# Recurrence: masked copies into a zeroed tile, and the decayed keys on VectorE

## The chip, the core and the metric

The program runs on one core of a Trainium2 chip. The metric is the device time of one execution in microseconds (us); of several executions the median is given. The engines of the core are TensorE (PE in the profile, PEld its weight loads), VectorE (DVE), ScalarE (ACT), GpSimd (POOL) and SyncE (SP, which here issues DMAs).

## The reference

Two transformer blocks on 512 tokens of width 1024, all in float32. The change lies in one of the three branches of the second block, a gated recurrence with four heads of 128 keys and 128 values (`hgrn2_mixer`):

```
b = jnp.cumsum(lfc, axis=2)
o_inter = jnp.einsum('bhck,bhkv->bhcv', qc * jnp.exp(b), state)
diff = b[:, :, :, None, :] - b[:, :, None, :, :]
decay = jnp.exp(jnp.where(causal, diff, NEG_BIG))
attn = jnp.einsum('bhtk,bhsk,bhtsk->bhts', qc, kc, decay)
o_intra = jnp.einsum('bhts,bhsv->bhtv', attn, vc)
```

Here `lfc` is the logarithm of the forget gate. The score `attn` of a token t with an earlier token s sums over keys a product of query, key and the decay between s and t. The reference goes in chunks of 64; the kernel takes chunks of 128.

## The kernel before

The decay between two tokens can't be split into a factor of t and a factor of s that are both safe to compute over a whole chunk. So the kernel splits the 128 x 128 scores of a chunk by seven levels (blocks of 2, 4, ... 128 tokens): at each level the pairs with s in the first half of a block and t in the second are exact with respect to the block's middle. An eighth part is the diagonal. Each pair (s, t) belongs to one level alone, so the scores are the sum over the eight parts, each under a mask of zeros and ones.

The class `Hgrn` does this. `mix` goes over 16 steps, one for each chunk i (4) and head h (4):

- `logs`: for two heads at a time, TensorE transposes the log gates, ScalarE and VectorE split them into a high and a low part (`fh`, `fl`).
- `decays`: TensorE multiplies them with a constant matrix `lev` (lines 1661 and 1662), ScalarE takes the exponential into `E`, nine tiles of 128 x 128 (line 1663). Tiles 0 to 6 times the keys are `yk` (GpSimd, line 1665); tile 8 times the keys is `kd` (line 1670); then tiles 0 to 7 are multiplied by the queries in place (VectorE, line 1672). Line 1672 overwrites what line 1665 reads, so it has to wait for it.
- `mixed`: TensorE forms the eight products (lines 1682 and 1684) into two PSUM tiles `s` of four each; VectorE multiplies each tile by its masks (line 1685) and adds the eight to one (lines 1686 to 1688) in the tile `am`.
- `put`: TensorE multiplies `am` with the values (line 1696), adds the state's part (line 1698), and the new state `hst` is formed (lines 1701 to 1709).

The steps overlap: while the `decays` of a step are computed, `mixed` works on the step before it and `put` on the one before that. The three PSUM tiles named `s` are shared with `scores` (lines 717 and 718), the indexer of another branch, which leaves its results on VectorE in `ixs` (lines 1313, 1316 and 1317). A generator `merge` hands out pieces of this and of projections (`pj`, lines 216 to 218, each weight split by ScalarE into `whi` and by VectorE into `wlo`, line 203) between the steps. After them `topk` (lines 1327 and 1328, 48 rounds of a maximum and a replacement on VectorE) selects the keys of another branch; its result is wanted only much later.

The order of each engine's instructions is set when the program is built, by a scheduler that goes by priorities and its own estimates. On the chip each engine takes its instructions in that order; semaphores make them wait for each other.

Of the kernel before, what the change touches and what calls it, by code (L numbers as in the profile page):

```python
# [10 lines left out]
F32 = mybir.dt.float32  # L11
F32R = mybir.dt.float32r
BF16 = mybir.dt.bfloat16
I32 = mybir.dt.int32
AF = mybir.ActivationFunctionType
ALU = mybir.AluOpType
AX = mybir.AxisListType
# [3 lines left out]
P = 128  # L21
# [13 lines left out]
class Net:  # L35
# [200 lines left out]
    def rsqrt(self, y, x, n, eng=None):  # L236

        eng = eng or self.nc.vector
        yi = self.t("rs_i", [P, 16], 3, I32)[:, :n]
        (self.nc.vector if eng is self.nc.scalar else eng).tensor_scalar(yi, x.bitcast(I32), -0.5, float(0x5F3759DF - 0x400000 - 2 ** 31), op0=ALU.mult, op1=ALU.add)  # L240
        u = yi.bitcast(F32)
        v = self.t("rs_t", [P, 16], 3)[:, :n]
        for it in range(3):
            o = y if it == 2 else u
            if eng is self.nc.scalar:
                eng.activation(v, u, AF.Identity, scale=u)
                eng.activation(v, v, AF.Identity, scale=x, bias=self.m15)
                eng.activation(o, v, AF.Identity, scale=u)
                continue
# [16 lines left out]
    def root(self, y, s, n, eps, x):  # L266

        nc = self.nc
        ln = nc.scalar.activation(y, s, AF.Ln, scale=1.0 / n, bias=self.eps[eps])
        self.after(ln, self.table)  # L270
        nc.scalar.activation(y, y, AF.Exp, scale=-0.5)
        nc.vector.tensor_scalar(x, s, -0.5 / n, -0.5 * eps, op0=ALU.mult, op1=ALU.add)
# [32 lines left out]
    def layernorm(self, x, g, b, eps, mv, sums=True):  # L305

        nc = self.nc
        if sums:
            nc.vector.tensor_scalar(mv[:, 2:3], mv[:, 0:1], mv[:, 1:2], -1.0 / D, op0=ALU.add, op1=ALU.mult)
            sq = self.wa([P, D], BF16)  # L310
            nc.scalar.activation(sq, x, AF.Square, bias=mv[:, 2:3], accum_out=mv[:, 3:4])
            self.root(mv[:, 5:6], mv[:, 3:4], D, eps, mv[:, 4:5])
# [639 lines left out]
    def tables2(self, tab):  # L952

        nc, a = self.nc, self.a
        pi = self.wp(dt=I32)
        nc.scalar.dma_start(pi, a["positions_2"].broadcast_to([P, S]))
# [23 lines left out]
    def bias2(self, pool):  # L980
# [1 line left out]


        nc, a = self.nc, self.a
        U32 = mybir.dt.uint32
        self.bias = [self.dr.tile([P, 4, (i + 1) * P], F32, name=f"bias{i}") for i in range(NT)]
        slot = lambda dt=F32, shape=None: pool.tile(shape or [P, S], dt, name=self.nm("bt"), tag="bt", bufs=6)
        hot = lambda: pool.tile([P, S], F32R, name=self.nm("bh"), tag="bh", bufs=2)
# [1 line left out]
        pos = a["positions_2"]  # L990
        pi = slot(I32)
        nc.sync.dma_start(pi, pos.broadcast_to([P, S]))
        qi = self.t("b_qi", [P, 3, NT], 1, I32)
        nc.sync.dma_start(qi[:, 0], pos[0].rearrange("(t p) -> p t", p=P))
# [10 lines left out]
        ps = self.p("s")  # L1005
# [9 lines left out]
        def part(src, op, arg, out):  # L1015
            k = slot(I32)[:, :src.shape[1]]
            nc.vector.tensor_single_scalar(k, src, arg, op=op)
            nc.vector.tensor_copy(out, k)
            return out
# [8 lines left out]
        for h in range(4):  # L1028
            raw = pool.tile([P, 2, 256], F32, name=self.nm("bo"), tag="bo", bufs=3)
            x = tab[h]  # L1030
            nc.sync.dma_start(raw, bass.AP(x.tensor, x.offset, [[1, P], [P, 2], [1, 256]]))
            f = self.split(raw.rearrange("p a b -> p (a b)"), slot)
            for r in range(2):
                ps = self.p("s")
                for k, y in enumerate((0, 0, 1, 1)):
                    z = k % 2
# [27 lines left out]
        for i in range(NT):  # L1064
            w = (i + 1) * P
            ps = pool.tile([P, 4 * S], F32, name=self.nm("bq"), tag="bq")
# [522 lines left out]
class Hgrn:  # L1589


    def __init__(self, net, hT, col):
        self.net, self.nc, self.hT, self.col = net, net.nc, hT, col
        nc, a = net.nc, net.a
        self.la, self.l1, self.kc, self.gb = net.bounds
        self.lev = net.sub.tile([P, 9, P], F32R, name="lev", tag="lev")
        nc.gpsimd.dma_start(self.lev, a["c_lev"])
        self.lmask = net.sub.tile([P, 8, P], BF16, name="lmask", tag="lmask")
        nc.gpsimd.dma_start(self.lmask, a["c_lmask"])
        self.bi = net.bi  # L1600
        self.f = net.sub.tile([P, 4, S], F32, name="hf", tag="hf")
        self.kT = []
# [34 lines left out]
    def mix(self, qT):  # L1637

        net, nc = self.net, self.nc
        kT, lev, lmask = self.kT, self.lev, self.lmask  # L1640
        st = [None] * 4
        self.os = [net.slot(shape=[P, 4, P]) for _ in range(4)]
        bq = lambda x, ti, n: x[:, ti].rearrange("p (o t) -> p o t", o=1).broadcast_to([P, n, P])
        pvs = {}

        def logs(i, hp):
            ti = slice(i * P, (i + 1) * P)
            pt = net.p("tr", [P, 4, P])[:, 0:2]
            for h in range(2):
                nc.tensor.transpose(pt[:, h, :], self.f[:, hp + h, ti], net.ident)  # L1650
            fh, fl = (self.w(t, [P, 2, P], 2, F32R) for t in ("fh", "fl"))
            nc.scalar.copy(fh, pt)
            nc.vector.tensor_sub(fl, pt, fh)
            return fh, fl

        def decays(i, h, fh, fl):
            ti = slice(i * P, (i + 1) * P)
            E = self.E()
            for c in range(0, 9, 3):
                ps = net.p("s", [P, 4, P])[:, :3, :]  # L1660
                nc.tensor.matmul(ps, lhsT=fh[:, h % 2, :], rhs=lev[:, c:c + 3, :], start=True, stop=False)
                nc.tensor.matmul(ps, lhsT=fl[:, h % 2, :], rhs=lev[:, c:c + 3, :], start=False, stop=True)
                nc.scalar.activation(E[:, c:c + 3, :], ps, AF.Exp)
            yk = self.w("yk", [P, 7, P], 2)
            nc.gpsimd.tensor_mul(yk, E[:, :7, :], bq(kT[h], ti, 7))
            kd = dec = None
            if i < NT - 1:
                kd = self.w("kd", [P, 2, P], 2)
                dec = net.t("hdec", [P, 1], 4)
                nc.vector.tensor_mul(kd[:, 0, :], E[:, 8, :], kT[h][:, ti])  # L1670
                nc.vector.tensor_copy(dec, E[:, 7, 127:128])
            nc.vector.tensor_mul(E[:, :8, :], E[:, :8, :], bq(qT[h], ti, 8))
            return E, yk, kd, dec

        def mixed(i, h, E, yk, kd, dec):
            ti = slice(i * P, (i + 1) * P)
            am = [self.w("am", [P, 4, P], 4) for _ in range(2)]
            for c in (0, 4):
                ps = net.p("s", [P, 4, P])
                for l in range(4):  # L1680
                    if c + l < 7:
                        nc.tensor.matmul(ps[:, l, :], lhsT=yk[:, c + l, :], rhs=E[:, c + l, :], start=True, stop=True)
                    else:
                        nc.tensor.matmul(ps[:, l, :], lhsT=kT[h][:, ti], rhs=qT[h][:, ti], start=True, stop=True)
                nc.vector.tensor_mul(am[c // 4], ps, lmask[:, c:c + 4, :])
            nc.vector.tensor_add(am[0], am[0], am[1])
            nc.vector.tensor_add(am[0][:, 0:2], am[0][:, 0:2], am[0][:, 2:4])
            nc.vector.tensor_add(am[0][:, 0], am[0][:, 0], am[0][:, 1])
            return i, h, E, am[0], kd, dec

        def put(i, h, E, am, kd, dec):
            if h == 0:
                pvs[i] = net.p("pv", [P, 4, P])
            pv = pvs[i]
            vv = self.bi[:, i, h * P:(h + 1) * P]
            nc.tensor.matmul(pv[:, h, :], lhsT=am[:, 0], rhs=vv, start=True, stop=i == 0)
            if i > 0:
                nc.tensor.matmul(pv[:, h, :], lhsT=E[:, 7, :], rhs=st[h], start=False, stop=True)
            if i < NT - 1:
                p2 = net.p("tr", [P, 4, P])  # L1700
                nc.tensor.transpose(p2[:, 0, :], kd[:, 0, :], net.ident)
                nc.scalar.copy(kd[:, 1, :], p2[:, 0, :])
                p3 = p2[:, 1, :]
                nc.tensor.matmul(p3, lhsT=kd[:, 1, :], rhs=vv, start=True, stop=True)
                new = self.w("hst", [P, P], 5)
                if i == 0:
                    nc.vector.tensor_copy(new, p3)
                else:
                    nc.vector.scalar_tensor_tensor(new, st[h], dec, p3, op0=ALU.mult, op1=ALU.add)
                st[h] = new  # L1710
            if h == 3:
                for j in range(4):
                    nc.scalar.copy(self.os[j][:, i], pv[:, j])

        held = prods = None
        f = logs(0, 0)
        for i in range(NT):
            for h in range(4):
                if h % 2 == 0:
                    g = f  # L1720
                d = decays(i, h, *g)
                if held:
                    m = mixed(*held)
                    if prods:
                        put(*prods)
                    prods = m
                held = (i, h) + d
                if h % 2 == 0 and (i, h) < (NT - 1, 2):
                    f = logs(i + h // 2, 2 - h)
                yield  # L1730
        m = mixed(*held)
        put(*prods)
        put(*m)
        yield
# [95 lines left out]
```

## Time and profile before

| | |
|---|---|
| time, median of 3 runs | 1677.36 us (1676.02 to 1679.92) |
| the profiled execution's own time | 1676.82 us |
| its span in the profile | 1675.1 us |
| granted clock of TensorE, mean | 0.995 of full speed |
| TensorE busy | 1618.9 us, 97% of the span |
| VectorE busy | 1056.8 us, 63% |
| ScalarE busy | 734.6 us, 44% |
| GpSimd busy | 105.7 us, 6% |

TensorE is busy nearly all the time, so the time of the kernel is TensorE's work and its waits. Shares over the whole span say little of one stage: the recurrence runs from about 770 to 906 us of the span, and there the other engines are loaded quite otherwise.

### The profile page before, as it was taken

How to read it: one execution, taken by the hardware profiler on the slowest of the kernel's cores; microseconds unless marked ns; L12 is line 12 of the kernel's file. 1: busy time of each engine (PE TensorE's matmuls, PEld its weight loads, DVE VectorE, ACT ScalarE, POOL GpSimd, SP SyncE). 2: the span in 40 equal slices, each digit the busy share in tenths (PEclk: the TensorE clock that was granted, in tenths of full speed). 3: DMA queues.
4: the chain of work that ended last, by engine and by line, in shares of the span. 5: the costliest groups of instructions: out<-in, count | busy, mean ns of one | idle time of the engine just before them, and what ended most of it. 6: DMA issues, size and time to landing. Idle time of an engine off the chain costs nothing.

```text
span 1675.1 us, 24263 instructions
## 1 busy us (share of the span) xinstructions
PE 1618.9 (97%) x9320; PEld 1374.6 (82%) x9320; DVE 1056.8 (63%) x2281; ACT 734.6 (44%) x1507; POOL 105.7 (6%) x131
## 2 busy tenths in 40 slices
PE   6999999999999999899889999999999999999997
PEld 6878797987787889787778866788889988888997
DVE  7686779784578796747999995624355444343233
ACT  4455664443465643465443765522233222222222
POOL 1021000000000000002221001100000000000000
PEclk9999999999999999999999999999999999999999
DMA  7453032341121414332011320223432533333321
GB/s 229 141 167 109 26 116 74 101 152 51 51 76 39 148 55 126 121 100 64 26 30 49 93 76 27 91 91 108 144 120 101 176 101 101 101 101 95 95 90 62
DMA packets 141883, 160.06 MB, mean 96 GB/s; under 512 B 14100, under 2 KB 131108, under 8 KB 141256
## 3 DMA queue, kind: packets, MB, share of 16 engines
q1 hardware_dynamic: 135960, 141.34, 28.0%
q0 software_dynamic: 2944, 11.86, 2.1%
q10 hardware_dynamic: 2864, 5.32, 1.0%
q8 instruction: 73, 1.20, 0.3%
q14 instruction: 42, 0.34, 0.1%
HBM read 143.55 MB, written 15.21 MB: 95 GB/s over the span
## 4 chain that ended last, share of the span: by engine, by line
PE 76%; DVE 13%; ACT 3%; issue 2%; DMA 1%; POOL 1%; ACTq 0%; POOLq 0%
PE pj L217 18%; PE pj L218 18%; PE pj L216 18%; PE pv L1093 3%; PE s L216 2%; PE s L217 2%; PE s L218 2%; PE tr L731 2%; DVE wlo L203 2%; PE s L717 1%; PE s L836 1%; PE s L718 1%; DVE ixs L1313 1%; DMA wraw<-in_w_in_dram 1%; ACT whi L202 1%
## 5 line engine op out<-in xcount | busy, mean ns | idle before, releaser
L216 PE MATMUL pj<-hTh,whi 128*128 128x512 f32 (+1 forms) x1136 | 440.5, 388 | 0.0
L217 PE MATMUL pj<-hTl,whi 128*128 128x512 f32 (+1 forms) x1136 | 440.3, 388 | 0.0
L218 PE MATMUL pj<-hTh,wlo 128*128 128x512 f32 (+1 forms) x1136 | 439.8, 388 | 0.3 <-DVE wlo L203 0.3
L203 DVE TENSOR_TENSOR wlo<-wraw,whi 128x1024 fp32r<-128x1024 f32 (+3 forms) x237 | 271.9, 1153 | 240.1 <-ACT whi L202 236.3
L202 ACT CAST whi<-wraw 128x1024 fp32r<-128x1024 f32 (+3 forms) x237 | 229.1, 980 | 327.1 <-PE pj L217 193.5
L216 PEld LDWEIGHTS pj<-hTh,whi 128*128 128x128 f32 x1136 | 213.6, 188 | 45.4 <-issue 6.6
L217 PEld LDWEIGHTS pj<-hTl,whi 128*128 128x128 f32 x1136 | 213.6, 188 | 43.4 <-issue 4.7
L218 PEld LDWEIGHTS pj<-hTh,wlo 128*128 128x128 f32 x1136 | 213.6, 188 | 43.2 <-issue 3.8
L216 PE MATMUL pj<-whi,hTh 128*128 128x256 f32 (+2 forms) x352 | 101.1, 289 | 3.4 <-ACT whi L207 2.7
L218 PE MATMUL pj<-whi,hTl 128*128 128x256 f32 (+2 forms) x352 | 102.5, 292 | 0.0
L217 PE MATMUL pj<-wlo,hTh 128*128 128x256 f32 (+2 forms) x352 | 101.2, 288 | 0.0
L217 PE MATMUL pj<-wlo,t2k 128*128 128x256 f32 x304 | 85.9, 283 | 0.0
L218 PE MATMUL pj<-whi,t2k 128*128 128x256 f32 x304 | 85.7, 282 | 0.0
L216 PE MATMUL pj<-whi,t2k 128*128 128x256 f32 x304 | 85.3, 281 | 0.0
L216 PE MATMUL s<-whi,t2k 128*128 128x256 f32 x264 | 73.8, 280 | 0.0
L218 PE MATMUL s<-whi,t2k 128*128 128x256 f32 x264 | 73.8, 280 | 0.0
L217 PE MATMUL s<-wlo,t2k 128*128 128x256 f32 x264 | 73.8, 280 | 0.0
L216 PEld LDWEIGHTS pj<-whi,hTh 128*128 128x128 f32 x352 | 68.2, 194 | 5.1 <-ACT whi L207 3.3
L217 PEld LDWEIGHTS pj<-wlo,hTh 128*128 128x128 f32 x352 | 68.4, 194 | 0.5 <-DVE wlo L203 0.2
L218 PEld LDWEIGHTS pj<-whi,hTl 128*128 128x128 f32 x352 | 68.3, 194 | 0.4
L734 ACT COPY wa<-tr 128x128 f32<-128x128 f32 (+3 forms) x96 | 40.7, 424 | 58.8 <-PE tr L731 57.4
L722 DVE CUSTOM_DVE_ANT_0 wa<-s,mask 128x128 f32<-128x128 f32 (+3 forms) x112 | 52.5, 485 | 11.4 <-PE tr L731 7.9
(455 smaller groups left out, 3120.2 us busy)
## 6 DMA issues: line engine op xcount, KB each, us to landing
wraw<-in_w_in_dram SPq DMA_DIRECT2D x112, 512.0 KB, 3.8
wraw<-in_w_ffn_gate_dram SPq DMA_DIRECT2D x22, 512.0 KB, 3.9
wraw<-in_w_ffn_up_dram SPq DMA_DIRECT2D x22, 512.0 KB, 4.6
wraw<-in_w_ffn_down_dram SPq DMA_DIRECT2D x16, 512.0 KB, 3.6
tok<-hres SPq DMA_DIRECT2D x12, 512.0 KB, 7.7
wraw<-in_w_out_dram SPq DMA_DIRECT2D x12, 512.0 KB, 4.3
hres<-tok SPq DMA_DIRECT2D x12, 512.0 KB, 2.7
wraw<-in_w_out_dram SPq DMA_DIRECT2D x8, 384.0 KB, 3.0
```

What stands on the lines that cost most here:

```text
L202: nc.scalar.copy(hi[:, ka:kb], raw)
L203: nc.vector.tensor_sub(lo[:, ka:kb], raw, hi[:, ka:kb])
L216: nc.tensor.matmul(out, lhsT=wh(k), rhs=xh(k), start=start and k == 0, stop=False)
L217: nc.tensor.matmul(out, lhsT=wh(k), rhs=xl(k), start=False, stop=False)
L218: nc.tensor.matmul(out, lhsT=wl(k), rhs=xh(k), start=False, stop=stop and k == nk - 1)
L717: nc.tensor.matmul(sc, lhsT=stacked[:, rows], rhs=twice[hh][:, cols], start=True, stop=False)
L718: return nc.tensor.matmul(sc, lhsT=stacked[:, rows], rhs=twice[2 + hh][:, cols], start=False, stop=stop)
L722: self.nc.vector.tensor_tensor_reduce(p[:, :w], sc[:, :w], self.maskw[:, S - w:] if mask is None else mask, scale=1.0, scalar=3e38, op0=AL ...
L731: x = nc.tensor.transpose(pt[:, j, :], src[:, j * P:(j + 1) * P], self.ident)
L734: nc.scalar.copy(dst[:, :n, :], pt[:, :n, :])
L836: last = nc.tensor.matmul(sc[:, S - wj:], lhsT=m, rhs=y[:, end - wj:end], start=n == 0, stop=n == len(todo) - 1)
L1093: x = self.nc.tensor.matmul(out, lhsT=l, rhs=r, start=k == 0, stop=k == i)
```

## The change

Two things are changed. First, VectorE no longer multiplies the products by masks and adds two tiles of four. It copies the products under the masks into a tile of zeros: two fixed tiles `am`, set to zero once by GpSimd, take turns from step to step. A place (s, t) in them is always written at the same level, so that what is not written stays zero. The second copy goes into the same tile as the first, and the first of the three additions (512 columns) falls away; the other two now write to `ay` and `az`. The masks are kept in float32 and not in bfloat16, and are read as integers. Second, line 1665 is given to VectorE.

```
-        self.lmask = net.sub.tile([P, 8, P], BF16, name="lmask", tag="lmask")
+        self.lmask = net.sub.tile([P, 8, P], F32, name="lmask", tag="lmask")
+        self.am = [net.sub.tile([P, 4, P], F32, name=f"am{j}", tag=f"am{j}") for j in range(2)]
+        for x in self.am:
+            nc.gpsimd.memset(x, 0.0)
...
-            nc.gpsimd.tensor_mul(yk, E[:, :7, :], bq(kT[h], ti, 7))
+            nc.vector.tensor_mul(yk, E[:, :7, :], bq(kT[h], ti, 7))
...
-            am = [self.w("am", [P, 4, P], 4) for _ in range(2)]
+            am = self.am[(i * 4 + h) % 2]
...
-                nc.vector.tensor_mul(am[c // 4], ps, lmask[:, c:c + 4, :])
-            nc.vector.tensor_add(am[0], am[0], am[1])
-            nc.vector.tensor_add(am[0][:, 0:2], am[0][:, 0:2], am[0][:, 2:4])
-            nc.vector.tensor_add(am[0][:, 0], am[0][:, 0], am[0][:, 1])
-            return i, h, E, am[0], kd, dec
+
+                nc.vector.copy_predicated(am, lmask[:, c:c + 4, :].bitcast(U32), ps)
+            y = self.w("ay", [P, 2, P], 1)
+            z = self.w("az", [P, 1, P], 3)
+            nc.vector.tensor_add(y, am[:, 0:2], am[:, 2:4])
+            nc.vector.tensor_add(z[:, 0], y[:, 0], y[:, 1])
+            return i, h, E, z, kd, dec
```

VectorE has as many instructions as before, GpSimd 16 products fewer and two fills more. The scheduler also puts other instructions in another order.

The first place is VectorE's queue in an early step of the recurrence. A row gives the line, the operation, the tile written, the tiles read and the size; the numbers behind the names are those of buffers. Before:

```order
L1671 COPY hdec_7890<-E_7874 128x1
L1685 TENSOR_TENSOR am_7894<-s_7896,lmask 128x512
L1313 SCALAR_TENSOR_TENSOR ixs_7860<-wa_7871,iw_6746,ixs_7860 128x384
L1670 TENSOR_TENSOR kd_7889<-E_7874,t2k_7493 128x128
L1672 TENSOR_TENSOR E_7874<-E_7874,t2k_7571 128x1024
L1685 TENSOR_TENSOR am_7895<-s_7902,lmask 128x512
L1707 COPY hst_7916<-tr_7912 128x128
L1686 TENSOR_TENSOR am_7894<-am_7894,am_7895 128x512
L1316 TENSOR_SCALAR ixs_7918<-wa_7922,iw_6746 128x384
L1687 TENSOR_TENSOR am_7894<-am_7894 128x256
L1317 SCALAR_TENSOR_TENSOR ixs_7918<-wa_7922,iw_6746,mask 128x128
L1688 TENSOR_TENSOR am_7894<-am_7894 128x128
```

And of the change, whose line numbers are up to five higher there:

```order
L1668 TENSOR_TENSOR yk_7889<-E_7876,t2k_7497 128x896
L1673 TENSOR_TENSOR kd_7891<-E_7876,t2k_7497 128x128
L1674 COPY hdec_7892<-E_7876 128x1
L1689 COPY_PREDICATED am_7281<-lmask,s_7896 128x512
L1675 TENSOR_TENSOR E_7876<-E_7876,t2k_7575 128x1024
L1689 COPY_PREDICATED am_7281<-lmask,s_7902 128x512
L1712 COPY hst_7917<-tr_7913 128x128
L1692 TENSOR_TENSOR ay_7908<-am_7281 128x256
L1316 TENSOR_SCALAR ixs_7919<-wa_7923,iw_6746 128x384
L1693 TENSOR_TENSOR az_7909<-ay_7908 128x128
L1317 SCALAR_TENSOR_TENSOR ixs_7919<-wa_7923,iw_6746,mask 128x128
```

`yk` now stands at the head of the step, and `kd` has moved up behind it, so that both stand ahead of the first masked copy; the addition of 512 columns is gone.

The second place is VectorE's queue near the end of the recurrence, where rounds of `topk` (MAX and MATCH_REPLACE) stand between the steps. Before:

```order
L1688 TENSOR_TENSOR am_8676<-am_8676 128x128
L1328 MATCH_REPLACE ixs_7794<-ixm_10085,ixs_7794 128x256
L1327 MAX ixm_10104<-ixs_7794 128x8
L1328 MATCH_REPLACE ixs_7794<-ixm_10104,ixs_7794 128x256
L1327 MAX ixm_10185<-ixs_7794 128x8
L1328 MATCH_REPLACE ixs_7794<-ixm_10185,ixs_7794 128x256
L1327 MAX ixm_10213<-ixs_7794 128x8
L1328 MATCH_REPLACE ixs_7794<-ixm_10213,ixs_7794 128x256
L1327 MAX ixm_10234<-ixs_7794 128x8
L203 TENSOR_TENSOR wlo_8941<-wraw_8942,whi_8940 128x1024
L1742 SCALAR_TENSOR_TENSOR t2k_8730<-t2k_8730,pj_8705 128x512
L1685 TENSOR_TENSOR am_8749<-s_8751,lmask 128x512
```

And of the change:

```order
L1693 TENSOR_TENSOR az_8681<-ay_8680 128x128
L1327 MAX ixm_9919<-ixs_7797 128x8
L1328 MATCH_REPLACE ixs_7797<-ixm_9919,ixs_7797 128x256
L1327 MAX ixm_9935<-ixs_7797 128x8
L1328 MATCH_REPLACE ixs_7797<-ixm_9935,ixs_7797 128x256
L1327 MAX ixm_9952<-ixs_7797 128x8
L1328 MATCH_REPLACE ixs_7797<-ixm_9952,ixs_7797 128x256
L1327 MAX ixm_9969<-ixs_7797 128x8
L1328 MATCH_REPLACE ixs_7797<-ixm_9969,ixs_7797 128x256
L1327 MAX ixm_10028<-ixs_7797 128x8
L204 TENSOR_TENSOR wlo_8929<-wraw_8930,whi_8928 128x1024
L1747 SCALAR_TENSOR_TENSOR t2k_8721<-t2k_8721,pj_8696 128x512
```

Before, eleven of the 48 rounds begin ahead of the last masked product; of the change five begin ahead of the last masked copy, the first of them at this place. Six rounds have moved behind the recurrence.

## Rows read from the trace of the kernel before

**Rows 1.** Page, part 1: busy us (share of the span) xinstructions.
```profile
PE 1618.9 (97%) x9320; PEld 1374.6 (82%) x9320; DVE 1056.8 (63%) x2281; ACT 734.6 (44%) x1507; POOL 105.7 (6%) x131
```
**Rows 2.** Busy time by engine in three stretches, the recurrence first.
```profile
core 0: us, PE busy (x) PEld busy (x) DVE busy (x) ACT busy (x) POOL busy (x), PEclk, DMA share, GB/s
780.00:900.00 120.00, 104.76 (x627) 87.89 (x625) 111.57 (x197) 51.15 (x115) 33.90 (x14) 1.00 0.12 32
900.00:1000.00 100.00, 98.05 (x585) 84.35 (x585) 97.05 (x249) 66.75 (x190) 3.31 (x4) 1.00 0.28 81
1000.00:1100.00 100.00, 98.97 (x496) 71.31 (x496) 55.12 (x171) 47.49 (x134) 11.19 (x12) 1.00 0.18 56
```
**Rows 3.** TensorE's waits, 780 to 902 us: us in total, times, longest.
```profile
PE pv L1696 <- DVE hdec L1671: 3.1, 2, 1.9
PE s L717 <- DVE am L1685: 2.6, 2, 1.4
PE s L1661 <- DVE am L1685: 2.2, 3, 0.9
PE tr L1650 <- DVE hst L1709: 2.0, 2, 1.5
PE s L1682 <- DVE E L1672: 1.9, 2, 1.1
PE tr L1701 <- DVE fl L1653: 1.6, 1, 1.6
PE pv L1696 <- DVE am L1688: 1.6, 1, 1.6
...
```
**Rows 4.** VectorE's waits, 760 to 910 us (two of five groups).
```profile
DVE E L1672 <- POOL yk L1665: 7.0, 6, 2.0
DVE kd L1670 <- ACT E L1663: 0.8, 2, 0.4
```
**Rows 5.** Timeline from 808 us: start, us, engine, instruction, [idle before it <-releaser].
```profile
808.29 2.47 POOL L1665 TENSOR_TENSOR yk<-E,t2k 128x896 f32<-128x896 f32 x1 [3.56 <-ACT E L1663]
808.73 2.44 DVE L1313 SCALAR_TENSOR_TENSOR ixs<-wa,iw,ixs 128x384 f32<-128x384 f32 x1
811.44 0.41 DVE L1653 TENSOR_TENSOR fl<-tr,fh 128x256 fp32r<-128x256 f32 x1
811.90 0.33 PE L1701 MATMUL tr<-ident,kd 128*128 128x128 f32 x1 [1.57 <-DVE fl L1653]
811.97 0.60 DVE L1313 SCALAR_TENSOR_TENSOR ixs<-wa,iw,ixs 128x384 f32<-128x384 f32 x1
```
**Rows 6.** Groups by shape, VectorE, 765 to 910 us: xcount | busy us, mean ns | idle before.
```profile
L1685 DVE TENSOR_TENSOR am<-s,lmask 128x512 f32<-128x512 f32 x32 | 21.6, 680 | 0.2
L1672 DVE TENSOR_TENSOR E<-E,t2k 128x1024 f32<-128x1024 f32 x16 | 19.5, 1218 | 7.0 <-POOL yk L1665 7.0
L203 DVE TENSOR_TENSOR wlo<-wraw,whi 128x1024 fp32r<-128x1024 f32 x10 | 13.5, 1353 | 5.6 <-ACT whi L202 5.5
L1686 DVE TENSOR_TENSOR am<-am,am 128x512 f32<-128x512 f32 x16 | 12.3, 771 | 0.0
L1313 DVE SCALAR_TENSOR_TENSOR ixs<-wa,iw,ixs 128x384 f32<-128x384 f32 x7 | 9.8, 1402 | 0.0
L1313 DVE SCALAR_TENSOR_TENSOR ixs<-wa,iw,ixs 128x256 f32<-128x256 f32 x7 | 8.9, 1274 | 0.0
L1327 DVE MAX8 ixm<-ixs 128x8 f32<-128x256 f32 x13 | 5.5, 426 | 0.3
L1328 DVE MATCH_REPLACE8 ixs<-ixm,ixs 128x256 f32<-128x256 f32 x12 | 4.9, 409 | 0.0
```
**Rows 7.** Timeline of VectorE: a single line 1313 of 256 columns.
```profile
805.60 0.47 DVE L1313 SCALAR_TENSOR_TENSOR ixs<-wa,iw,ixs 128x256 f32<-128x256 f32 x1
```
**Rows 8.** Groups by shape, VectorE, whole span: masked copies of another stage.
```profile
L1072 DVE COPY_PREDICATED bo<-b_n,bq 128x512 f32<-128x512 uint32 x4 | 2.7, 747 | 0.0
```
**Rows 9.** Timeline of VectorE from 125 us: three of these copies in a row.
```profile
125.40 2.00 DVE L1072 COPY_PREDICATED bo<-b_n,bq 128x512 f32<-128x512 uint32 x3
```

More of the change, by code (lines that the diff above doesn't have):

```diff
@@ L14 @@
 I32 = mybir.dt.int32
+U32 = mybir.dt.uint32
 AF = mybir.ActivationFunctionType
@@ L984, in bias2 @@
         nc, a = self.nc, self.a
-        U32 = mybir.dt.uint32
         self.bias = [self.dr.tile([P, 4, (i + 1) * P], F32, name=f"bias{i}") for i in range(NT)]
```

## The prediction

> **What bounds the kernel now.** I read the page first: TensorE is busy for 97% of the span, VectorE for 63% [rows 1]. So only what makes TensorE wait can be worth anything, and I looked for the stretches where it does. The windows show one inside the span: from 780 to 900 us, most of the recurrence, TensorE is busy for 104.8 of 120 us, so it idles 15.2, while VectorE is busy for 111.6 [rows 2]. In the 100 us behind it TensorE idles only 2.0, although VectorE is busy for 97.0 there, and in the 100 after that VectorE is half idle. In the recurrence, then, VectorE is the engine that TensorE waits for, and the waits say so themselves: all of the groups in the stretch name VectorE as the releaser, and the seven shown add up to 15.0 us [rows 3]. They name different lines (`hdec`, `am`, `hst`, `E`, `fl`). That is the mark of an engine that is late as a whole, whatever stands in its queue when TensorE asks.
>
> Then I asked why VectorE is late, and its groups by shape gave a second answer besides its load. Line 1313 has a mean of 1402 ns for 384 columns and of 1274 ns for 256 [rows 6]; single ones of these shapes take 0.60 [rows 5] and 0.47 us [rows 7]. The timeline shows what stretches them: at 808.73 one of 384 columns starts while GpSimd is at work on `yk`, and takes 2.44 us, that is, it ends shortly after GpSimd does at 810.76; `fl` behind it is late, and TensorE waits 1.57 us for `fl` [rows 5]. Besides, VectorE waits 7.0 us outright for `yk`, since line 1672 overwrites what GpSimd still reads [rows 4].
>
> **The change, part by part.** All of it lies between 770 and 906 us; sums are for the 16 steps.
>
> The addition of 512 columns goes. It is 16 instructions with a mean of 771 ns: 12.3 us off VectorE [rows 6]. Of these 1.5 us are holds by GpSimd, measured against 680 ns of the masked product of as many columns.
>
> GpSimd's products go, and with them the holds and the waits. The holds of the other groups: line 1313, 7 x (1402 - 600) = 5.6 us and 7 x (1274 - 470) = 5.6 us; line 203, 10 x (1353 - 1218) = 1.4 us, with line 1672, of as many columns, for the normal length [rows 5 to 7]. Together 12.6 us. With the 7.0 us of waits for `yk` [rows 4] VectorE gets 19.6 us back here.
>
> `yk` comes onto VectorE: 896 columns, two inputs in SBUF. Between the 680 ns for 512 columns and the 1218 ns for 1024 [rows 6], a line gives 680 + 384 x 538 / 512 = 1083 ns, so 17.3 us for 16. This is a price from both sides, and I give it no range of its own.
>
> The masked products become masked copies, 32 of them. The trace has this operation elsewhere, at the same width with all operands in SBUF: 747 ns on the mean [rows 8], and 2.00 us for three in a row, or 0.67 each [rows 9]. The source is now in PSUM, which no row shows for this operation; the masked product reads the same tile from PSUM in 680 ns, as if it cost nothing. Against 680 ns the 32 copies change the sum by -0.3 to +2.1 us. I take 0, by the copies in a row, since VectorE's queue is full here too.
>
> Masks of four bytes in place of two, and two fills by GpSimd: the masks are loaded and the tiles filled before the recurrence, while GpSimd has nothing else to do and TensorE goes on with projections, and I put it at nothing. Were that cover gone, it would be a few us, once.
>
> So VectorE's account is -12.3 - 19.6 + 17.3 = -14.6 us (-14.9 to -12.5), against 15.2 us for which TensorE idles. This is the core of the forecast: the engine that is late becomes earlier by nearly as much as it makes the other wait.
>
> Here the Trainium skill has a rule that speaks against the change. Its page "Perfetto Trace Analysis", section "Optimizing Scalar/DVE Operations", says that when the vector engine is saturated, moving work to ScalarE or even GpSimd may make sense, and adds that the two share a read port, so that it might not help. By its first half the change gives work back to a full engine, -12.3 + 17.3 = +5.0 us, and the time would come to 1682. The page "SBUF — State Buffer", section "Who interferes with whom", says that the shared port is held for a whole instruction and the other engine blocks fully; the instruction at 808.73 agrees with that. The sums above don't use either.
>
> **What TensorE gets of it.** Not all 14.6. First, by what is left of the load: VectorE's busy time from 780 to 900 falls by about 12.3 + 12.6 - 17.3 = 7.6 us to 104, and six rounds of `topk`, each 426 + 409 ns [rows 6], move behind the recurrence, so 99, against TensorE's 104.8. Two queues that are so nearly equal and wait for each other leave some idle time. Its bounds: the 2% of the stretch behind, with VectorE as full [rows 2], give 2 us; 13% as now give 15. I take 5 us, a third of today's, nearer to the low end because TensorE's present waits come each from a hold or wait of 1 to 2 us that disappears. I followed all 15 back in the timeline as in [rows 5]; 13 have one just ahead of them. That gives 15.2 - 5 = 10.2 us.
>
> Second, the six rounds, 5.0 us, now load a stretch in which VectorE has 3.0 us free; what doesn't fit runs over into the next, where it has 45 [rows 2], and nothing urgent waits for `topk`. I set 0.5 us for work of VectorE that stands behind these rounds in the queue and is awaited.
>
> Third, the new order itself: the first masked copy of a step now stands behind `yk` and `kd`. I count that in the 5 us.
>
> 10.2 - 0.5 = 9.7 us. The profiled execution took 1676.8 us, of which 1675.1 are the span, so 1667.1; the median lies 0.5 above this execution: **1667.5 us**.
>
> **Rivals.** *All of it comes back.* TensorE idles for 2 us in the recurrence, as in the stretch behind it, and a little is won as its pipeline drains less often: 14 to 16 us, 1662. For it: the holds are the larger half of VectorE's lateness. Against it: 99 us of work in about 107 is still 93%.
>
> *VectorE stays the late engine; no change.* `yk` now waits in VectorE's own queue for the exponentials; on GpSimd that wait was free, and it was long (3.56 us of idle time before the `yk` of [rows 5]). While VectorE waits at its head, everything behind it waits too. For about 0.8 us in each step, 13 us would go. Against it: `hdec` and `kd` stood in the same queue before and read the same tile, and VectorE waited for `E` only 0.8 us in all [rows 4]. The time would be 1676.
>
> *Slower: the tiles `s`.* The first masked copy of a step comes later by `yk` and `kd`, and until it has run TensorE can't have that PSUM tile again; there are three. The waits for them are 2.6 + 2.2 us in five cases today [rows 3]. If in each step TensorE stood still for all of `yk`, that is 16 x 1.08 = 17.3 us; with copies at 747 ns 2.1 more. Against the 15.2 won, that gives +4 us: 1681. It decides from 15.2 / 16 = 0.95 us a step. Against it: in between, TensorE has projections to do, which the new order puts there in larger number. The rule of the saturated engine, +5.0 us with the holds left out of account, ends in the same place by another way, 1682; the trace bears it out least, as VectorE demonstrably stands still under GpSimd's products.
>
> **How the numbers follow.** Forecast (5 to 14 us faster) 0.62; all of it 0.12; no change 0.15; slower 0.11, of which the saturated engine 0.03. The measurement can tell about 0.2%, or 3.4 us, from no change. Faster by more is the first two, 0.74; within it 0.15; slower 0.11. The likeliest case alone spans 1663 to 1672. The range has to take in most of the case without change and part of the case in which all comes back: 1661 to 1677. It leaves out the slower case and the outermost of the others.
>
> **What would show it right or wrong.** In the profile after: `yk` on VectorE at 1.0 to 1.15 us; masked copies at 0.66 to 0.75; lines 1313 at 0.60 and 0.47 us throughout, with no instruction of VectorE near 2 us; no wait for `yk`; VectorE busy for about 100 us of the 120 that begin at 780; TensorE idle for about 5 us in the recurrence, which ends some 10 us earlier; TensorE's idle time behind it as before. I am wrong if copies from PSUM take a microsecond and more, if TensorE's waits for `am` (tiles `s`) grow to 15 us, if VectorE stands before `yk` waiting for ScalarE's `E`, or if the displaced `topk` makes TensorE wait past 906 us.

## The result: 1.1% faster, 1660.4 us

The changed kernel takes 1660.37 us (median of four runs, 1657.14 to 1661.47), the kernel before 1678.44 us beside it. The ratio is 0.9891, with a 95% interval of 0.9871 to 0.9910: 18 us faster. The forecast was 1667.5 us with a range from 1661 to 1677, so the time lies just below the range. The direction was right, the size too small. The profiled execution took 1661.47 us (span 1659.7), which is 15.3 us less than the 1676.8 of before.

Part 1 of the page of the changed kernel answers to [rows 1]:

```profile
PE 1618.0 (97%) x9320; PEld 1374.3 (83%) x9320; DVE 1045.5 (63%) x2281; ACT 734.5 (44%) x1507; POOL 67.0 (4%) x117
```

TensorE has the same work, and VectorE does 11 us less although it took over 16 products. The windows of the changed kernel over the same stretches as [rows 2], the recurrence first:

```profile
core 0: us, PE busy (x) PEld busy (x) DVE busy (x) ACT busy (x) POOL busy (x), PEclk, DMA share, GB/s
780.00:900.00 120.00, 119.86 (x769) 104.42 (x768) 112.49 (x227) 57.30 (x141) 0.00 (x0) 1.00 0.14 41
900.00:1000.00 100.00, 98.15 (x511) 77.63 (x509) 94.48 (x250) 66.70 (x185) 2.28 (x4) 0.98 0.24 71
1000.00:1100.00 100.00, 99.47 (x501) 75.01 (x502) 49.56 (x144) 44.80 (x117) 11.02 (x12) 1.00 0.23 72
```

From 780 to 900 us TensorE idles for 0.14 us, where it was 15.2. Its list of waits over the stretch of [rows 3] is empty. The stretch behind idles as before (1.85 and 1.95 us), so the stall didn't move there. Its granted clock is 0.98 where it was 1.00: in this trace TensorE ran at 0.50 (1.2 GHz) from 965 to 968 us, behind a wait of 1.9 us for ScalarE's `ms`. The kernel before has a wait of 1.8 us there and kept 1.00.

A fixed window holds a different part of the program once the stage is shorter. For the comparisons from here on I take the stage itself, from the first matmul on `lev` to the last of `put` (line 1696, now 1701). One row of the windows view for the kernel before, columns as above:

```profile
769.70:906.20 136.50, 121.19 (x736) 103.06 (x736) 124.73 (x225) 55.86 (x125) 38.33 (x16) 1.00 0.14 39
```

And the same row for the changed kernel:

```profile
770.60:890.40 119.80, 119.66 (x742) 103.11 (x741) 110.45 (x208) 56.01 (x125) 0.00 (x0) 1.00 0.15 45
```

The stage is 16.7 us shorter: TensorE's idle time in it falls from 15.31 (136.50 - 121.19) to 0.14, and its own work there takes 1.5 us less. The stage begins 0.9 us later, and what follows it takes 0.4 us longer, together 15.4 us off the span. Note VectorE: 124.73 of 136.50 is 91%, 110.45 of 119.80 is 92%. It is as full as before, and TensorE no longer waits.

VectorE's groups by shape in the changed kernel, 765 to 910 us, for [rows 6]:

```profile
L1689 DVE COPY_PREDICATED am<-lmask,s 128x512 f32<-128x512 uint32 x32 | 23.6, 742 | 0.7 <-PE s L1685 0.6
L1675 DVE TENSOR_TENSOR E<-E,t2k 128x1024 f32<-128x1024 f32 x16 | 19.5, 1216 | 0.0
L1668 DVE TENSOR_TENSOR yk<-E,t2k 128x896 f32<-128x896 f32 x16 | 17.4, 1090 | 0.9 <-ACT E L1666 0.8
L204 DVE TENSOR_TENSOR wlo<-wraw,whi 128x1024 fp32r<-128x1024 f32 x12 | 14.7, 1225 | 5.6 <-ACT whi L203 5.6
...
L1313 DVE SCALAR_TENSOR_TENSOR ixs<-wa,iw,ixs 128x384 f32<-128x384 f32 x7 | 4.3, 611 | 0.0
...
L1327 DVE MAX8 ixm<-ixs 128x8 f32<-128x256 f32 x8 | 3.4, 429 | 0.2
L1313 DVE SCALAR_TENSOR_TENSOR ixs<-wa,iw,ixs 128x256 f32<-128x256 f32 x7 | 3.4, 485 | 0.0
...
L1328 DVE MATCH_REPLACE8 ixs<-ixm,ixs 128x256 f32<-128x256 f32 x7 | 2.9, 418 | 0.0
```

Line 1313 is down to 611 and 485 ns from 1402 and 1274, line 204 (203 before) to 1225 from 1353, and the 7.0 us of waiting ahead of `E` are 0.0. A masked copy from PSUM has its first price: 742 ns, against 680 for the product in its place.

VectorE's timeline at the place of [rows 5], in the changed kernel:

```profile
808.35 0.61 DVE L1313 SCALAR_TENSOR_TENSOR ixs<-wa,iw,ixs 128x384 f32<-128x384 f32 x1
808.88 1.08 DVE L1668 TENSOR_TENSOR yk<-E,t2k 128x896 f32<-128x896 f32 x1
809.96 0.29 DVE L1673 TENSOR_TENSOR kd<-E,t2k 128x128 f32<-128x128 f32 x1
810.17 0.14 DVE L1674 COPY hdec<-E 128x1 f32<-128x1 f32 x1
810.24 0.74 DVE L1689 COPY_PREDICATED am<-lmask,s 128x512 f32<-128x512 uint32 x1
810.87 1.21 DVE L1675 TENSOR_TENSOR E<-E,t2k 128x1024 f32<-128x1024 f32 x1
```

In the 2.44 us that line 1313 alone took, VectorE now does line 1313, `yk`, `kd`, `hdec` and most of a masked copy.

### The profile page after: what moved, and what is told of

It reads as the page before. It is cut to its first block, busy times and chain, and to the rows that moved or that the text cites. A ratio compares the mean times of both kernels' runs of the same rounds, so it can differ in the third digit from the quotient of the medians.

```text
span 1659.7 us, 24221 instructions
## 1 busy us (share of the span) xinstructions
PE 1618.0 (97%) x9320; PEld 1374.3 (83%) x9320; DVE 1045.5 (63%) x2281; ACT 734.5 (44%) x1507; POOL 67.0 (4%) x117
## 4 chain that ended last, share of the span: by engine, by line
PE 83%; DVE 8%; ACT 2%; DMA 1%; issue 1%; ACTq 0%; DVEq 0%
PE pj L218 19%; PE pj L217 19%; PE pj L219 19%; PE pv L1093 3%; PE tr L732 2%; PE s L217 2%; PE s L218 2%; PE s L219 2%; PE s L718 2%; PE s L1685 2%; PE s L719 1%; PE s L837 1%; DVE wlo L204 1%; DMA wraw<-in_w_in_dram 1%; PE pv L848 1%
```

## The experiments

Two things left VectorE at once: the time that GpSimd's products cost it (holds of 15.1 us in nine instructions, by each one's length above the shortest of its kind; a tenth, the only one of its kind, a line 1316 of 256 columns, took 2.17 us and takes 0.34 in the changed kernel; and the 7.0 us of [rows 4]) and the addition of 512 columns. My first theory, A, was that GpSimd's products are what matters; its rival, B, that VectorE's load as a whole is. The letters are explained in each expectation. Times are medians, ratios are against the kernel before on the same chip, and the stage is that of the section above.

**Half of the change: `yk` alone.** The kernel before, with one word changed:

```diff
-            nc.gpsimd.tensor_mul(yk, E[:, :7, :], bq(kT[h], ti, 7))
+            nc.vector.tensor_mul(yk, E[:, :7, :], bq(kT[h], ti, 7))
```

> Edit: of the change, only the keys' product goes to VectorE; masked products and all three additions stay as before. Theory A (single holds: TensorE's waits in the recurrence come from the 1 to 2 us that VectorE stands still under each of GpSimd's products; without them even a nearly full VectorE keeps up): the holds (14.1 us) and the waits (7.0 us) are gone, VectorE has the addition of 512 columns more per step than in the change, so a few us of TensorE's idle time are left, 2 to 5; time 1662 to 1666. Theory B (load: only VectorE's account counts, which is -14.1 - 7.0 + 17.3 = -3.8 us here): 1674 to 1676.

Measured: 1668.46 us, ratio 0.9952 (0.9937 to 0.9967). It lies between the two, nearer to A: putting 17 us of work on the engine that TensorE waits for makes the kernel 0.5% faster. Here the Trainium skill's advice is answered ("Perfetto Trace Analysis", section "Optimizing Scalar/DVE Operations": with a saturated vector engine, offloading even to GpSimd may make sense, but the two share a read port). The run goes against the first half and with the caution. The stage of this kernel:

```profile
770.40:899.80 129.40, 124.79 (x750) 106.33 (x750) 118.23 (x218) 56.26 (x125) 0.00 (x0) 0.99 0.13 37
```

TensorE still idles for 4.61 us, and its work in the stage takes 124.79 us instead of 119.66. Of these 5.1 us, 3.8 are also in the whole span (1621.8 against 1618.0 busy). The windows of this kernel show a part of them, in the column PEclk:

```profile
856.00:858.00 2.00, 1.11 (x4) 0.60 (x4) 2.00 (x6) 0.74 (x2) 0.00 (x0) 1.00 0.00 0
858.00:859.00 1.00, 0.12 (x1) 0.00 (x0) 1.00 (x2) 0.49 (x1) 0.00 (x0) 1.00 0.00 0
859.00:860.00 1.00, 0.86 (x4) 0.89 (x5) 1.00 (x3) 0.00 (x0) 0.00 (x0) 0.64 0.00 0
860.00:861.00 1.00, 1.00 (x6) 1.00 (x6) 1.00 (x2) 0.00 (x0) 0.00 (x0) 0.50 0.00 0
861.00:862.00 1.00, 1.00 (x7) 1.00 (x6) 1.00 (x3) 0.00 (x0) 0.00 (x0) 0.50 0.00 0
862.00:863.00 1.00, 1.00 (x7) 0.93 (x6) 1.00 (x2) 0.00 (x1) 0.00 (x0) 0.65 0.33 25
```

TensorE had been busy for 1.23 of 3 us, after three waits of 0.58, 0.58 and 1.02 us close together, and then ran at 0.50, that is at 1.2 GHz, for about three microseconds. The four rows that are not at 1.00 lack 0.36, 0.50, 0.50 and 0.35, or 1.7 us of full speed. The other 2.1 of the 3.8 us I can't assign. TensorE's waits in this stage name ScalarE for 2.5 us and VectorE for 1.6.

**The other half: copies alone.** The changed kernel, with the same word the other way:

```diff
-            nc.vector.tensor_mul(yk, E[:, :7, :], bq(kT[h], ti, 7))
+            nc.gpsimd.tensor_mul(yk, E[:, :7, :], bq(kT[h], ti, 7))
```

> Edit: of the change, only the masked copies into tiles of zeros; the keys' product stays on GpSimd. Theory A: holds and waits remain, most of TensorE's waits with them; a gain of 3 to 6 us, time 1672 to 1675. Theory B: VectorE's account is -12.3 for the addition, +2 for the copies at 742 ns, so -10 us, time 1667 to 1669.

Measured: 1673.59 us, ratio 0.9974 (0.9963 to 0.9986), as A said. Holds of 12.6 us in eight instructions remain, and 6.0 us of waits for `yk`. Its stage:

```profile
770.10:900.80 130.70, 120.42 (x725) 102.24 (x726) 116.66 (x225) 55.07 (x125) 37.13 (x16) 1.00 0.15 41
```

The halves gain 0.48% and 0.26% alone and 1.09% together. In TensorE's idle time there is nothing odd in that: 10.7 us and 5.0 us go alone, 15.2 together. What the first half doesn't get, it loses in TensorE's pace.

**One tile of zeros instead of two**, since the next experiments need its room:

```diff
-            am = self.am[(i * 4 + h) % 2]
+            am = self.am[0]
```

> Edit: the change with one tile of zeros in place of two, which frees room in SBUF for the next experiment; its control. Both theories: as the change, 1659 to 1662, since VectorE takes the additions of a step ahead of the next step's copies anyway.

Measured: 1659.47 us, ratio 0.9900 (0.9882 to 0.9919), TensorE idle for 0.15 us in the stage. The second tile does nothing for the time.

**GpSimd's holds put back, without its work.** On the kernel with one tile, each step gives GpSimd a product of 896 columns that nobody reads. The other engines' instructions stand in the same order as in the kernel with one tile:

```diff
+            nc.gpsimd.tensor_mul(self.w("junk", [P, 7, P], 1, BF16), lmask[:, :7, :], E[:, 8:9, :].broadcast_to([P, 7, P]))
```

> Edit: the control with one more product on GpSimd in each step, of 896 columns with two inputs in SBUF, started by the same exponential as the keys' product was before; it writes a tile that nobody reads and overwrites or delays no data of others, so that no instruction waits for it. TensorE, VectorE and ScalarE have the same instructions in the same order as the control. Theory A (holds by the two engines' sharing of SBUF): VectorE's instructions with two inputs in SBUF show lengths of 1.5 to 3 us again, TensorE idles for 5 to 12 us in the recurrence, time 1665 to 1672. Rival C (what stretched them before was the tile that both engines read, or the semaphores between them, not the mere overlap): as the control, 1660, no instruction stretched.

Measured: 1679.54 us, ratio 1.0013 (1.0004 to 1.0023): 20 us slower than its base, the whole gain of the change and more, from an engine whose results nobody waits for. I had expected too little. The stage of this kernel:

```profile
770.40:910.30 139.90, 124.08 (x750) 104.19 (x749) 136.10 (x213) 56.61 (x125) 39.07 (x16) 1.00 0.14 38
```

With the same 213 instructions as its base, VectorE's busy time is 136.10 us instead of 111.35. Its timeline shows one hold, under a product of GpSimd:

```profile
810.71 2.50 POOL L1669 TENSOR_TENSOR junk<-lmask,E 128x896 bf16<-128x896 f32 x1 [3.06 <-ACT E L1666]
810.67 0.60 DVE L1313 SCALAR_TENSOR_TENSOR ixs<-wa,iw,ixs 128x384 f32<-128x384 f32 x1
811.20 2.16 DVE L1694 TENSOR_TENSOR az<-ay 128x128 f32<-128x128 f32 x1
813.28 0.41 DVE L1656 TENSOR_TENSOR fl<-tr,fh 128x256 fp32r<-128x256 f32 x1
```

The addition `az` has 128 columns and takes 0.29 us elsewhere. It starts while GpSimd is at work and ends 0.15 us after it (813.36 and 813.21). So it is with all instructions with two inputs in SBUF that are held in the stage, in this kernel and in the others: with 128 columns they end 0.15 us after GpSimd's product, with 256 0.28, with 384 0.41 or 0.42, with 512 0.55, whenever they started ([rows 5]: 811.17 and 810.76). It looks as if they began only when GpSimd was done; the hold is then as long as what is left of GpSimd's product.

**GpSimd busy, but only writing.** The same base, with as many microseconds of GpSimd, nearly all of them fills:

```diff
+            junk = self.w("junk", [P, 7, P], 1, BF16)
+            nc.gpsimd.tensor_copy(junk[:, 0, :2], E[:, 8, :2])
+            for _ in range(3):
+                nc.gpsimd.memset(junk, 0.0)
```

> Edit: the control with one tile of zeros, and in each step GpSimd copies two columns of the exponential (so that it starts when the product of the hold experiment did) and then fills a spare tile of 896 columns three times; nobody waits for it. The order on TensorE, VectorE and ScalarE is that of the control. GpSimd is about as long at work, but reads next to nothing from SBUF. If what holds VectorE is GpSimd's reading: as the control, 1658 to 1661, no VectorE instruction stretched. If any work of GpSimd holds it: 1668 to 1680, as with the product.

Measured: 1660.95 us, ratio 0.9904 (0.9888 to 0.9921), as the base, with GpSimd busy for 49.07 us of the stage. VectorE's timeline in this kernel, while the three fills run from 806.24 to 808.89 us:

```profile
806.24 2.65 POOL L1672 MEMSET junk<- 128x896 bf16 x3
806.92 0.61 DVE L1313 SCALAR_TENSOR_TENSOR ixs<-wa,iw,ixs 128x384 f32<-128x384 f32 x1
807.45 1.09 DVE L1668 TENSOR_TENSOR yk<-E,t2k 128x896 f32<-128x896 f32 x1
808.53 0.29 DVE L1677 TENSOR_TENSOR kd<-E,t2k 128x128 f32<-128x128 f32 x1
```

All three of VectorE have their normal length. So it is GpSimd's reading that costs VectorE, not its being busy. What is held in the stage has two inputs in SBUF, but for line 1316, which reads one tile and one factor per partition: in the kernel with copies alone, eight masked copies (source in PSUM) start under a product of GpSimd and take 732 to 751 ns, and two of the additions `az` take 2.17 and 2.18 us. The Trainium skill says this in "SBUF — State Buffer", section "Who interferes with whom": a VectorE instruction with at most one SBUF input, outside the paired-port modes, does not contend with GpSimd. The traces agree for the masked copies; line 1316 may run in such a mode, since its 256 columns end 0.15 us after GpSimd's product, like 128 elsewhere, but no run tries it.

**The other product on GpSimd.** On the kernel with one tile, and with two tiles for `E` in place of three, VectorE makes the queries' product into a tile of its own, and GpSimd then the keys' product in place, so that GpSimd waits for VectorE and not the reverse:

```diff
+            Q = self.w("Q", [P, 8, P], 3)
+            nc.vector.tensor_mul(Q, E[:, :8, :], bq(qT[h], ti, 8))
+            nc.gpsimd.tensor_mul(E[:, :7, :], E[:, :7, :], bq(kT[h], ti, 7))
...
-            nc.vector.tensor_mul(E[:, :8, :], E[:, :8, :], bq(qT[h], ti, 8))
```

> Edit: masked copies into one tile of zeros, keys' product on GpSimd as before the change, but GpSimd now multiplies the keys in place and VectorE writes the queries' product to a tile of its own; so GpSimd waits for VectorE and VectorE never for GpSimd. It differs from the run with the copies only by who waits. Theory A1 (the holds make most of TensorE's waits): 1669 to 1674, little better than that run. Theory A2 (VectorE's waits for the keys' product do): 1661 to 1665.

Measured: 1673.01 us, ratio 0.9980 (0.9963 to 0.9997). That is the time of A1. No wait for GpSimd is left on VectorE, but holds of 18.2 us in fifteen instructions are, as much as the holds and waits of the run with the copies together (12.6 + 6.0), and TensorE idles for 12.2 us in the stage. So the run doesn't price the two apart: what VectorE no longer waits, it is held longer. It also differs from that run in the tiles for `E` and in the order. That the wait is the smaller part rests on the kernel before: 7.0 us against 15.1 of holds.

**More work for VectorE, with GpSimd away.** The changed kernel, with the addition of 256 columns done twice, three times and six times in each step (three kernels, with 2, 3 and 6 in this line):

```diff
-            nc.vector.tensor_add(y, am[:, 0:2], am[:, 2:4])
+            for _ in range(3):
+                nc.vector.tensor_add(y, am[:, 0:2], am[:, 2:4])
```

Three times:

> Edit: the change, with the addition of 256 columns done three times in each step (the same sums again), that is some 10.6 us more of VectorE's queue in the recurrence and no work for GpSimd. My prediction left 5 us of TensorE's idle time to VectorE's mean load of 93%; the run of the change showed 0.1. Theory A (VectorE has slack as long as it has no single stand of 1 to 2 us): TensorE idles for 1 to 3 us, time 1661 to 1664. Theory B (VectorE's mean load): the account is as that of 512 columns added again, nearly no slack left, 1666 to 1671.

Twice and six times:

> The change with the addition of 256 columns done twice in each step instead of once: 16 more instructions of about 0.42 us, 6.8 us more on VectorE in the recurrence; the output is the same. VectorE is idle for 9.3 us there in the changed kernel, and TensorE for 0.1. Theory A, a threshold: TensorE hides VectorE's work until VectorE's own idle time in the stage is used up. 6.8 fits into 9.3, so 1660 to 1662, TensorE idle for under 1 us in the stage. Theory B, every microsecond costs: tripling the addition (+13.6 us) cost 8, so 0.6 for each; +6.8 costs 4: 1663.5 to 1666, TensorE idle for 2 to 4 us.

> The change with the addition of 256 columns done six times in each step: 34 us more on VectorE in the recurrence; the output is the same. VectorE alone would then take 110 + 34 = 144 us for a stage of 120. Theory A, a threshold at VectorE's idle time: 34 - 9 = 25 us slower than the change, 1685, less what the scheduler moves out of the stage (the rounds of topk, up to 5 us): 1679 to 1686. Theory B, 0.6 for each microsecond throughout: 1660 + 20 = 1678 to 1682. A time under 1672 would show that the scheduler finds other work for TensorE and that VectorE's load is not what decides here.

Measured: 1663.92 us for twice (ratio 0.9924, 0.9907 to 0.9940), 1668.42 for three times (0.9947, 0.9930 to 0.9964) and 1693.57 for six times (1.0096, 1.0078 to 1.0114). The 6.8, 13.6 and 34 us of the expectations are sums of lengths, and the lengths of neighbours overlap: VectorE's busy time in the stage rises by 5.5, 10.3 and 28.4 us over the changed kernel's. Twice and three times met theory B, and there is no threshold at VectorE's idle time: the first 5.5 us already cost 3.5, although 9.3 would have fitted. Six times met neither theory: the last 18 us cost 25, more than they are. (The scheduler also puts some of TensorE's instructions in another order in these three, as it does in the two halves. TensorE's waits name ScalarE for 1.4 of 2.6 us with the addition done twice and for 2.7 of 4.4 with three times, so it isn't VectorE alone that comes last there.) The stage with six additions:

```profile
770.10:924.00 153.90, 136.37 (x763) 114.74 (x763) 138.86 (x297) 57.23 (x125) 0.00 (x0) 0.92 0.13 35
```

TensorE idles for 17.5 us and its work in the stage takes 136.37 instead of 119.66. Much of these 16.7 us goes with the granted clock, which lacks (1 - 0.92) x 153.9 = 12.3 us of full speed over the stage, a part of it while TensorE idled. It fell in these two windows, the second of which ends behind the stage:

```profile
840.00:880.00 40.00, 32.19 (x142) 26.16 (x142) 32.64 (x68) 13.12 (x31) 0.00 (x0) 0.74 0.05 14
920.00:940.00 20.00, 15.38 (x106) 14.95 (x107) 18.92 (x59) 9.28 (x38) 0.00 (x0) 0.75 0.10 30
```

**Holds ahead of the stage.** The changed kernel has other copies on GpSimd, in `twice`, which hold VectorE for 5.4 us in 19 instructions before the recurrence:

```diff
-            nc.gpsimd.tensor_copy(u[rest], u[own])
+            nc.vector.tensor_copy(u[rest], u[own])
```

> Edit: the change, and in the first block's attention the copy of 512 columns over half of the partitions that GpSimd does for each head pair (it reads SBUF as well) goes to VectorE, 32 copies. Theory A: the holds on VectorE of 150 to 450 ns each there (5.0 us in 17 cases) are gone, and TensorE's waits behind them, 3.4 us in 8 cases, fall to 0 to 1.5; against it stand 32 copies of some 0.35 us on a queue that is not full there. Time 1657 to 1659. Theory B (VectorE's load counts): 1660 to 1664.

Measured: 1659.88 us, ratio 0.9893 (0.9877 to 0.9910), the time of the change, which lies between the two theories' ranges. The holds shrink to 0.3 us in two instructions and VectorE is busy 7.6 us longer (1053.1 against 1045.5 in the span), yet TensorE's idle time ahead of the stage stays (28.35 and 28.44 us). Its waits for line 711 fall from 3.2 us in seven cases to 1.9 in three, and others grow. The run removes holds and adds load at once, and the order changes with it, so it gives neither a price of its own; together they are worth nothing there.

## Why the prediction was right on the direction and too small

The table puts the kernels in the order of VectorE's time in the stage: its busy time, holds included, and its waits for GpSimd. TensorE's idle time is the stage's length less its busy time; all are from rows like those above. TensorE's busy time contains work at the lower clock in `yk` alone and with the addition three and six times.

| kernel | VectorE busy + waits for GpSimd | TensorE busy | TensorE idle |
|---|---|---|---|
| changed | 110.4 | 119.7 | 0.14 |
| addition twice | 116.0 | 121.5 | 3.0 |
| `yk` alone | 118.2 | 124.8 | 4.6 |
| addition three times | 120.8 | 125.5 | 4.8 |
| copies alone | 116.7 + 6.0 = 122.7 | 120.4 | 10.3 |
| other product on GpSimd | 124.2 | 121.8 | 12.2 |
| before | 124.7 + 7.0 = 131.7 | 121.2 | 15.3 |
| GpSimd's reading put back | 136.1 | 124.1 | 15.8 |
| addition six times | 138.9 | 136.4 | 17.5 |

The columns of VectorE's time and TensorE's idle time rise together, whether the time is VectorE's own work, a hold or a wait. TensorE has about 120 us of work of its own in the stage. With VectorE's 110 it waits for nothing, from about 116 on it does. By the table A and B were both halves: the holds were the larger item, but added work costs as well. Cause and effect are shown purely in one pair alone, GpSimd's reading put back against the kernel with one tile (VectorE 111.4 us, TensorE idle for 0.15): there the order of VectorE, TensorE and ScalarE is the same. Between the other kernels TensorE's order differs too, and a longer stage takes in more rounds of `topk` (225 VectorE instructions before, 208 after), so what the order is worth by itself is not shown.

Step by step:

- *Addition of 512 columns, -12.3 us; holds and waits, -19.6 us; `yk`, +17.3 us.* Right as far as they go. The holds and the waits for `yk` are gone entirely, and `yk` takes 17.4 us at 1090 ns (1083 expected).
- *Masked copies at nothing.* Mis-sized: 742 instead of 680 ns, 32 x 62 = 2.0 us, the upper bound given. By the terms VectorE's account is then -12.6 rather than -14.6 us. The profiles give more: 11.3 us less busy time in the whole span and 7.0 of waits, -18.3. Holds that the terms left out make 2.8 of the 5.7 between (line 1316: 2.17 us to 0.34; `kd`: 12 x (372 - 289) ns); the rest isn't assigned.
- *Masks and fills at nothing.* The stage begins 0.9 us later, which is all that they can have cost.
- ***"I take 5 us, a third of today's."*** This is the step that failed: 0.14 us was left, with VectorE still 92% busy. The 5 us came from two comparisons. The first set VectorE's 99 us from 780 to 900 us against TensorE's 104.8, that is 5.8 apart ("two queues that are so nearly equal and wait for each other leave some idle time"). That window cuts off both ends of the stage. Over all of it the same terms give VectorE 124.7 - 7.6 - 5.0 = 112.1 us against 121.2, which is 9.1 apart, and 9.2 was measured (110.45 and 119.66). In the table the three kernels whose VectorE lies 4.7 to 6.6 us under TensorE's work idle for 3.0 to 4.8 us: the 5 us fits the distance that I compared, not the one that the stage has. The second comparison, by shares of the stretch (2% and 13%), says nothing, since VectorE's share is 91% before and 92% after. That a few microseconds of this distance decide is read from the table; the one pair with the same order goes all the way from 9.2 under to 12 over.
- *0.5 us for the six displaced rounds of `topk`.* Nothing of the kind: behind the stage TensorE's only listed wait up to 1010 us is 1.9 us for ScalarE's `ms`.
- *The account of the difference.* The profiled execution was to gain 9.7 us and gained 15.3. The idle time makes 4.9 of the 5.6 between, the rounds 0.5, TensorE's quicker work in the stage 1.5, less 1.3 lost ahead of and behind it, where the clock fell from 965 us. The median was to lie 0.5 above the profiled execution and lies 1.1 below it, which makes the remaining 1.6 of 7.1.

The signs: `yk` and the copies fell into their bands, and no instruction of VectorE came near 2 us. VectorE's "about 100 of 120" from 780 us was wrong as stated, 112.49, since 10 us of that window now lie behind the stage, where VectorE is full.

The rivals: "all of it comes back" was the case, at 1662 and a chance of 0.12; the argument against it, that VectorE would still be 93% full, is the one that failed. No change, by `yk` waiting for the exponentials: VectorE waited 0.8 us for them in all, with or without the move. Slower, by the tiles `s`: the list has no wait for `am`. Slower, by the saturated engine: `yk` alone on VectorE refutes it. The case in which all of it comes back, priced at 14 to 16 us, lay inside the range, at its low end. It kept 2 us of idle time, as in the stretch behind, where 0.14 was left, and the median against the profiled execution made another 1.6; these two put the time below the range.

## What to carry to other kernels

When one engine makes another wait, compare times over the stage, not shares: the late engine's whole time (work, holds, waits) against the other's own work there. Take the whole stage, not a window that cuts it. Here all of the wait came back when the first fell 9 us of 120 under the second; in three kernels where it lay 5 to 7 us under it, 3 to 5 us of idle time were left. Before giving VectorE's work to GpSimd, look at lengths by shape: one operation that takes 2.4 us here and 0.6 there is paying for it.

## What the runs showed of the hardware

A product on GpSimd that reads SBUF cost more on VectorE than it saved: 39 us of it, with results that nobody uses, made the kernel 20 us slower, while 49 us of mere fills cost nothing measurable. What is held ends a fixed time after GpSimd's product, which depends on its columns alone, as if it began only then. A masked copy of 128x512 from PSUM takes 742 ns, 62 more than a product.

I hadn't expected TensorE's clock to enter. In the kernel before, with 15.3 us of idle time, the stage's granted clock is 1.00; with `yk` alone, and only 4.6 us of it, TensorE fell to 0.50 around 860 us, where three waits stood within 4 us. With GpSimd's reading put back, the clock stays at 1.00 with 15.8 us of idle time as well. How the waits lie may count as much as their sum; no run varied it alone.
